# Raw weights of the second down block of a pair in four plain tiles of 128x512 instead of two tiles of 128x1024

## The chip, the cores and the metric

The kernel runs on one core of a Trainium2 chip. The metric is device time in microseconds (us), the median of several runs; lower is better. The engines are TensorE (PE in the profile, its weight loads PEld), VectorE (DVE), ScalarE (ACT), GpSimd (POOL) and SyncE (SP), which here only issues DMAs.

## The reference

Two transformer layers on 512 tokens of width 1024, in fp32. Each layer has a mixing part (layer 0: chunked spatial gating; layer 1: attention with forgetting over 12 heads; both beside an attention over 256 memory rows), and then a feed-forward part with 2816 hidden columns, which is what matters here:

```
f = rmsnorm(h, ln_ffn_pre[layer])
f = (silu(f @ w_ffn_gate[layer]) * (f @ w_ffn_up[layer])) @ w_ffn_down[layer]
h = h + rmsnorm(f, ln_ffn_post[layer])
```

## The kernel before

Every fp32 matrix product is made of three matmuls. An operand is split into a high part (`whi`, a cast to fp32r by ScalarE) and a low part (`wlo`, the difference, by VectorE); `mm3` (L191 to L193) adds high x high, high x low and low x high in PSUM. The splits of L239 are the largest groups of ScalarE and VectorE.

The 22 hidden blocks of 128 columns of a layer are worked off as two in front and then five groups of four (`groups`). In a group, blocks go in pairs. A pair is a gate block and an up block, each of the class `Seven`: a 2x2 block product made of seven half-size products instead of eight, with sums of weights (L1040, L1042, L1044, L1045, on VectorE) before the products. A `Seven` loads its raw weights at L144 into two tiles of 128x1024 with the tag `raw`. Its products run in the order 1, 7, 6, 2, 5, 4, 3; product 1 goes to the PSUM tile `a`, product 7 to the tile `e` (tag `tr`, two banks), others to `x`, and ScalarE copies partial results from PSUM to PSUM at L1055. The ends of a gate block are sums on VectorE (L1083, L1084), a product with the row scale (L1171) and a Silu on ScalarE (L1172).

When the two pairs of a group are done, in the first four groups of a layer, `down_sevens` multiplies their 512 hidden columns with the down weights, again as products of seven: a `DownSeven` `a` for the first pair and a `DownSeven` `b` for the second. Results gather in the eight accumulators `ys` (plain tiles `y` of 128x512): by an addition on VectorE (`final`, L1265), or by a copy on ScalarE (`put`, L1260) and an accumulating DMA from GpSimd's queue (L1262, `y<-yo`). Sums of partial results between PSUM banks are copied by ScalarE (L1286). There are eight such stages in all, four in each layer. In the fifth group of a layer the down weights go through the ordinary tail, which is not part of the change.

The pools that matter:
- `raw`: four tiles of 128x1024 fp32, used in turn by every `Seven` (two each) and every `DownSeven` (two each);
- `y` (function `plain`): twelve tiles of 128x512 fp32. Eight are the accumulators; the other four hold nothing in the groups of layer 1 and, in layer 0, the raw memory rows `mem` for layer 1, which are loaded at L345 and read by ScalarE and VectorE (L243, L244) in the last group;
- the weight parts: eight tiles each of high and low parts, from which TensorE reads.

A `DownSeven` reads its raw weights for the sums L1235, L1237, L1239 and L1240 on VectorE, and cuts seven weight tiles into parts from them and the sums, each just ahead of its product. So a raw tile comes free when the last part is cut from it, in the middle of the stage. Both its loads stand in SyncE's queue, in which a load whose tile is not free holds up the loads behind it.

A planner orders the instructions of each engine at build time, by the order in which they are written and by costs that it assumes, with the waits on tiles and data; at run time each engine works its list off in order. The program text is thus a list of priorities, not the order of issue.

Of the kernel before, what the change touches and what calls it, by code (L numbers as in the profile page):

```python
# [7 lines left out]
F32 = mybir.dt.float32  # L8
# [7 lines left out]
P = 128  # L16
# [24 lines left out]
def hybrid(ctx: ExitStack, tc: tile.TileContext, i: dict, out: bass.AP):  # L41
    nc = tc.nc
# [4 lines left out]
    wp = ctx.enter_context(tc.tile_pool(name="weights", bufs=4))  # L47
# [5 lines left out]
    last_load, last_exp, last_parts = [None], [None], [None, None]  # L53

    def name(s):
        n_of[s] = n_of.get(s, 0) + 1
        return f"{s}_{n_of[s]}"
# [4 lines left out]
    def plain(s, shape=(P, T), dt=F32):  # L62
        return yp.tile(list(shape), dt, tag="y", name=name(s))

    def prob(s, shape=(P, T)):
        return tp.tile(list(shape), F32, tag="p", name=name(s), bufs=6)

    def temp(s, shape=(P, T), tag="t", bufs=4, dt=F32):
        return tp.tile(list(shape), dt, tag=tag, name=name(s), bufs=bufs)
# [4 lines left out]
    def ps(tag, shape=(P, T), s="ps"):  # L74
        return pp.tile(list(shape), F32, tag=tag, name=name(s), bufs=2 if tag == "tr" else 3)
# [1074 lines left out]
    def feed_forward(layer, phase, xp, meanwhile=None):  # L1150
# [43 lines left out]
        class Inner:  # L1194

            def __init__(self, k, aside):
                self.k, self.aside, self.u = k, aside, {}
# [22 lines left out]

        class DownSeven:

            def __init__(self, pair):
                self.x = pair.x
                raws = []
                for dh in range(2):
                    raw = wp.tile([P, 1024], F32, tag="raw", name=name("raw"), bufs=4)
                    last_load[0] = nc.sync.dma_start(
                        raw.rearrange("p (m c) -> p m c", m=4),
                        i["w_down"][layer, 4 * dh : 4 * dh + 4, :, pair.k : pair.k + 2, :].rearrange("m p k c -> p m (k c)"))  # L1230
                    raws.append(raw.rearrange("p (m k c) -> p m k c", m=4, k=2))
                a11, a12, a21, a22 = (r[:, :, x, :] for r in raws for x in range(2))
                self.w = {4: a22}
                s3 = temp("s3").rearrange("p (m c) -> p m c", m=4)
                V.tensor_sub(s3, a11, a21)  # L1235
                self.w[1] = self.parts(a11)
                V.tensor_add(a21, a21, a22)  # L1237
                self.w[2] = self.parts(a12)
                V.tensor_sub(a11, a11, a21)  # L1239
                V.tensor_add(a12, a11, a12)  # L1240
                self.w.update({3: a12, 5: a21, 6: a11, 7: s3})
# [14 lines left out]
        def down_sevens(pairs):  # L1256

            def put(x, *where):
                some = prob("yo")
                A.copy(some, x)  # L1260
                for tb, dh in where:
                    G.dma_start(ys[tb][dh], some, accum_op=ALU.add)  # L1262

            def final(x, tb, dh):
                V.tensor_add(ys[tb][dh], x, ys[tb][dh])  # L1265

            a, b = DownSeven(pairs[0]), None
            chain = [ps("lg", s="yc") for _ in range(2)]
            a.product(chain, 1, True, False)
            lows = [ps("mm", s="yl") for _ in range(2)]  # L1270
            a.product(lows, 2, True, False)
            shared = [ps(t, s="ys") for t in ("tr", "tr")]
            a.product(shared, 7, True, False)
            ups = [ps(t, s="yu") for t in ("mm", "lg")]
            a.product(ups, 3, True, False)
            b = DownSeven(pairs[1])
            b.product(chain, 1, False, True)
            for x in range(2):
                put(chain[x], (x, 0))
            b.product(shared, 7, False, True)  # L1280
            for x in range(2):
                put(shared[x], (x, 1), (x + 2, 1))
            for u in (a, b):
                u.product(chain, 6, False, u is b)
            for x in range(2):
                A.copy(shared[x], chain[x])  # L1286
            b.product(ups, 3, False, True)
            for x in range(2):
                final(ups[x], x + 2, 0)
            a.product(chain, 5, False, False)  # L1290
            a.product(shared, 4, False, False)
            b.product(lows, 2, False, True)
            for x in range(2):
                final(lows[x], x, 0)
            b.product(chain, 5, False, True)
            for x in range(2):
                put(chain[x], (x + 2, 0), (x + 2, 1))
            b.product(shared, 4, False, True)
            for x in range(2):
                final(shared[x], x, 1)  # L1300
# [11 lines left out]
        a, close = boundary(phase, G_MIX_POST + layer, G_FFN_PRE + layer, nnorm, rb, first, evac_first, scaled)  # L1312
# [12 lines left out]
        for gi, (k0, k1) in enumerate(groups):  # L1325
            fs, pairs = [], []
            for m in range(k0, k1, 2):
                if meanwhile and m == k1 - 2 and gi == len(groups) - 1:
                    next(meanwhile)
                if gi < len(groups) - 1:  # L1330
                    pairs.append(Inner(m, m < k1 - 2))
                else:
                    fs += [(act("fhi"), act("flo")) for _ in range(2)]
                Kind = FirstSeven if m == 2 else Seven
                sevens((lambda: Kind(xs, lambda n: i["w_gate"][layer, m + n], gate_rows),
                        lambda: Kind(xs, lambda n: i["w_up"][layer, m + n],
                                     lambda row, src, t: up_rows(row, src, t, fs, pairs and pairs[-1]))), m == 2, m == k0)
            nk = k1 - k0
            if gi == len(groups) - 1:
                if layer:  # L1340
                    with behind([gates[2]]):
                        A.preload_act_table_set("natural_log_exp_and_others")
                if meanwhile:
                    next(meanwhile)

                eps = small("eps")
                V.tensor_mul(eps, nnorm.r4, nnorm.r4)
                V.reciprocal(eps, eps)
                V.tensor_scalar_mul(eps, eps, RMS_EPS)
                return tail_of(fs, lambda kp, dh, aside, k0=k0: down_weights(layer, k0 + 2 * kp, dh, aside), ys, eps,  # L1350
                               layer == 1)
            down_sevens(pairs)
# [300 lines left out]
```

## Time and profile before

| | |
|---|---|
| time, median of 3 runs (lowest to highest) | 1120.58 us (1119.38 to 1121.08) |
| profiled execution | 1125.12 us; span 1123.4 us |
| mean granted TensorE clock | 0.989 |
| busy: TensorE, weight loads, VectorE, ScalarE, GpSimd | 1091.1, 995.8, 956.2, 760.7, 107.7 us |
| loads of down weights | 44 of 512 KB, 4.3 us from issue to landing (median) |
| accumulating DMAs y<-yo | 80 of 256 KB, 8.1 us (median) |
| loads of gate weights by a Seven or ahead | 44 of 512 KB, 4.0 us (median) |

A line of the groups or of the timeline names the source line, the engine, the operation, the tiles written and read (out<-in), the shapes and the count; in brackets, or behind the second bar, stands the idle time of the engine just before it and what ended that. A busy TensorE in the profile is not TensorE at its peak, since matmul ends are modelled. The windows give busy time by engine in the order TensorE, weight loads, VectorE, ScalarE, GpSimd, and then the granted clock, the DMA engines' busy share and GB/s.

### The profile page before, as it was taken

How to read it: one execution, taken by the hardware profiler on the slowest of the kernel's cores; microseconds unless marked ns; L12 is line 12 of the kernel's file. 1: busy time of each engine (PE TensorE's matmuls, PEld its weight loads, DVE VectorE, ACT ScalarE, POOL GpSimd, SP SyncE). 2: the span in 40 equal slices, each digit the busy share in tenths (PEclk: the TensorE clock that was granted, in tenths of full speed). 3: DMA queues.
4: the chain of work that ended last, by engine and by line, in shares of the span. 5: the costliest groups of instructions: out<-in, count | busy, mean ns of one | idle time of the engine just before them, and what ended most of it. 6: DMA issues, size and time to landing. Idle time of an engine off the chain costs nothing.

```text
span 1123.4 us, 19912 instructions
## 1 busy us (share of the span) xinstructions
PE 1091.1 (97%) x7267; PEld 995.8 (89%) x7267; DVE 956.2 (85%) x1906; ACT 760.7 (68%) x1588; POOL 107.7 (10%) x136
## 2 busy tenths in 40 slices
PE   9999999999999999899999999999999999999898
PEld 7998889998989899898988998889988989889896
DVE  7879769998989889896868889779998989979876
ACT  6776578666657657577646888788666657657464
POOL 0000000002030202101000000010012030202100
PEclk9999999999999999999999999999999999989999
DMA  7521331338475655755222555331238485644732
GB/s 264 152 85 57 113 113 39 114 93 208 131 174 163 142 141 130 171 167 155 76 76 76 153 138 139 100 113 39 94 77 211 127 182 157 150 132 120 181 95 76
DMA packets 77850, 143.85 MB, mean 128 GB/s; under 512 B 6772, under 2 KB 41608, under 8 KB 77752
## 3 DMA queue, kind: packets, MB, share of 16 engines
q1 hardware_dynamic: 63032, 116.57, 33.6%
q0 software_dynamic: 14016, 25.70, 13.3%
q8 instruction: 57, 0.93, 0.4%
q10 hardware_dynamic: 704, 0.32, 0.1%
q14 instruction: 41, 0.34, 0.1%
HBM read 105.23 MB, written 2.10 MB: 96 GB/s over the span
## 4 chain that ended last, share of the span: by engine, by line
PE 60%; DVE 18%; DMA 13%; issue 4%; ACT 4%; POOL 1%; DVEq 0%; SPq 0%; ACTq 0%
DVE wlo L239 6%; DMA raw<-in_w_gate 5%; PE y L191 4%; PE y L192 4%; PE y L193 4%; DMA y<-yo 4%; PE ps L191 4%; PE ps L193 4%; PE ps L192 4%; DMA raw<-in_w_down 3%; PE a L191 3%; PE a L193 2%; PE a L192 2%; PE v L191 2%; PE v L193 2%
## 5 line engine op out<-in xcount | busy, mean ns | idle before, releaser
L239 ACT CAST whi<-raw 128x512 fp32r<-128x512 f32 x492 | 293.1, 619 | 149.9 <-PE x L192 28.5
L239 DVE TENSOR_TENSOR wlo<-raw,whi 128x512 fp32r<-128x512 f32 x492 | 326.4, 684 | 30.9 <-ACT whi L239 29.3
L191 PE MATMUL a<-xshi,whi 128*128 128x256 f32 x320 | 90.8, 284 | 1.1 <-ACT e L1055 1.1
L191 PE MATMUL x<-xshi,whi 128*128 128x256 f32 x320 | 91.6, 286 | 0.3 <-ACT x L1055 0.3
L193 PE MATMUL x<-xshi,wlo 128*128 128x256 f32 x320 | 90.9, 284 | 0.0
L192 PE MATMUL x<-xslo,whi 128*128 128x256 f32 x320 | 90.9, 284 | 0.0
L193 PE MATMUL a<-xshi,wlo 128*128 128x256 f32 x320 | 90.0, 281 | 0.0
L192 PE MATMUL a<-xslo,whi 128*128 128x256 f32 x320 | 90.0, 281 | 0.0
L1262 POOL DMA_DIRECT2D y<-yo x80 | 69.6, 1263 | 210.9 <-ACT yo L1260 182.8
L191 PE MATMUL ps<-xshi,whi 128*128 128x256 f32 (+1 forms) x224 | 68.4, 305 | 0.0
L192 PE MATMUL ps<-xslo,whi 128*128 128x256 f32 (+1 forms) x224 | 66.6, 298 | 0.0
L193 PE MATMUL ps<-xshi,wlo 128*128 128x256 f32 (+1 forms) x224 | 66.3, 298 | 0.0
L191 PEld LDWEIGHTS a<-xshi,whi 128*128 128x128 f32 x320 | 60.6, 189 | 2.6 <-ACT e L1055 2.2
L191 PEld LDWEIGHTS x<-xshi,whi 128*128 128x128 f32 x320 | 61.8, 193 | 1.0 <-ACT x L1055 0.9
L192 PEld LDWEIGHTS x<-xslo,whi 128*128 128x128 f32 x320 | 61.5, 192 | 0.0
L193 PEld LDWEIGHTS x<-xshi,wlo 128*128 128x128 f32 x320 | 61.4, 192 | 0.0
L192 PEld LDWEIGHTS a<-xslo,whi 128*128 128x128 f32 x320 | 60.5, 189 | 0.4
L193 PEld LDWEIGHTS a<-xshi,wlo 128*128 128x128 f32 x320 | 60.4, 189 | 0.0
L1040 DVE TENSOR_TENSOR s<-raw,raw 128x512 f32<-128x512 f32 x40 | 27.5, 688 | 36.4 <-DMA raw<-in_w_gate 32.4
L191 PE MATMUL e<-t3hi,whi 128*128 128x256 f32 x160 | 46.0, 287 | 12.5 <-ACT whi L239 6.7
L191 PE MATMUL a<-d2hi,whi 128*128 128x256 f32 x160 | 48.2, 302 | 9.1 <-ACT x L1055 9.1
L239 ACT CAST whi<-s 128x512 fp32r<-128x512 f32 x56 | 34.8, 621 | 31.1 <-DVE s L1040 16.2
(359 smaller groups left out, 3598.4 us busy)
## 6 DMA issues: line engine op xcount, KB each, us to landing
raw<-in_w_gate SPq DMA_DIRECT2D x44, 512.0 KB, 4.0
raw<-in_w_up SPq DMA_DIRECT2D x44, 512.0 KB, 4.6
raw<-in_w_down SPq DMA_DIRECT2D x44, 512.0 KB, 4.3
y<-yo POOLq DMA_DIRECT2D x80, 256.0 KB, 8.1
raw<-in_w_out SPq DMA_DIRECT2D x16, 512.0 KB, 4.0
flo<-s POOLq DMA_DIRECT2D x16, 256.0 KB, 3.4
raw<-in_w_b_q SPq DMA_DIRECT2D x8, 512.0 KB, 4.8
raw<-in_w_a_v SPq DMA_DIRECT2D x6, 512.0 KB, 8.2
```

The lines of the kernel that those rows point to most:

```text
L191: PE.matmul(o, w[0], x[0], start=start, stop=False, skip_group_check=more)
L192: PE.matmul(o, w[0], x[1], start=False, stop=False, skip_group_check=more)
L193: return PE.matmul(o, w[1], x[0], start=False, stop=stop, skip_group_check=more)
L239: last_parts[:] = A.copy(hi, src), (eng or V).tensor_sub(lo, src, hi)
L1040: V.tensor_add(self.s3, a11, a21)
L1262: G.dma_start(ys[tb][dh], some, accum_op=ALU.add)
```

## The change

`DownSeven` takes a second argument. The first block of a stage loads as before: two loads of 512 KB into two `raw` tiles, in rows of 1 KB, with the two weight blocks of the pair interleaved. The second block takes four tiles `wd` from the pool `y` instead, one for each quarter of the weights (a11, a12, a21, a22), and fills them by four loads of 256 KB in rows of 512 bytes. All sums, splits and products stay, on tiles that are contiguous instead of strided.

```diff
         class DownSeven:
 
-            def __init__(self, pair):
+            def __init__(self, pair, spare):
                 self.x = pair.x
-                raws = []
-                for dh in range(2):
-                    raw = wp.tile([P, 1024], F32, tag="raw", name=name("raw"), bufs=4)
-                    last_load[0] = nc.sync.dma_start(
-                        raw.rearrange("p (m c) -> p m c", m=4),
-                        i["w_down"][layer, 4 * dh : 4 * dh + 4, :, pair.k : pair.k + 2, :].rearrange("m p k c -> p m (k c)"))
-                    raws.append(raw.rearrange("p (m k c) -> p m k c", m=4, k=2))
-                a11, a12, a21, a22 = (r[:, :, x, :] for r in raws for x in range(2))
+                if spare:
+                    a11, a12, a21, a22 = (plain("wd").rearrange("p (m c) -> p m c", m=4) for _ in range(4))
+                    for n, a in enumerate((a11, a12, a21, a22)):
+                        last_load[0] = nc.sync.dma_start(
+                            a, i["w_down"][layer, 4 * (n // 2) : 4 * (n // 2) + 4, :, pair.k + n % 2, :].rearrange("m p c -> p m c"))
+                else:
+                    raws = []
+                    for dh in range(2):
+                        ...
+                    a11, a12, a21, a22 = (r[:, :, x, :] for r in raws for x in range(2))
...
-            a, b = DownSeven(pairs[0]), None
+            a, b = DownSeven(pairs[0], False), None
...
-            b = DownSeven(pairs[1])
+            b = DownSeven(pairs[1], True)
```

More of the change, by code (lines that the diff above doesn't have):

```diff
@@ L1221, in feed_forward @@
         class DownSeven:
-            def __init__(self, pair):
+            def __init__(self, pair, spare):
                 self.x = pair.x
-                raws = []
-                for dh in range(2):
-                    raw = wp.tile([P, 1024], F32, tag="raw", name=name("raw"), bufs=4)
-                    last_load[0] = nc.sync.dma_start(
-                        raw.rearrange("p (m c) -> p m c", m=4),
-                        i["w_down"][layer, 4 * dh : 4 * dh + 4, :, pair.k : pair.k + 2, :].rearrange("m p k c -> p m (k c)"))
-                    raws.append(raw.rearrange("p (m k c) -> p m k c", m=4, k=2))
-                a11, a12, a21, a22 = (r[:, :, x, :] for r in raws for x in range(2))
+                if spare:
[6 more added lines that the diff above has]
+                    for dh in range(2):
+                        raw = wp.tile([P, 1024], F32, tag="raw", name=name("raw"), bufs=4)
+                        last_load[0] = nc.sync.dma_start(
+                            raw.rearrange("p (m c) -> p m c", m=4),
+                            i["w_down"][layer, 4 * dh : 4 * dh + 4, :, pair.k : pair.k + 2, :].rearrange("m p k c -> p m (k c)"))
+                        raws.append(raw.rearrange("p (m k c) -> p m k c", m=4, k=2))
+                    a11, a12, a21, a22 = (r[:, :, x, :] for r in raws for x in range(2))
                 self.w = {4: a22}
```

## The prediction

> **What bounds the kernel now.** I read the page first: its span and its chain of work that ended last, by engine.
>
> ```profile
> span 1123.4 us, 19912 instructions
> ...
> PE 60%; DVE 18%; DMA 13%; issue 4%; ACT 4%; POOL 1%; DVEq 0%; SPq 0%; ACTq 0%
> ```
>
> TensorE sets the time, but 18% of the chain is VectorE and 13% is DMA, which can only be places where TensorE stood still. So next: what TensorE waited for (columns: total us, times, longest).
>
> ```profile
> PE a L191 <- ACT x L1055: 9.1, 4, 3.0
> PE e L191 <- ACT whi L239: 6.7, 3, 2.6
> PE e L191 <- DVE y L1265: 5.8, 5, 2.0
> PE ys L192 <- DVE wlo L239: 1.9, 2, 1.5
> ```
>
> Tile e belongs to the second product of a gate block. Its eight waits (6.7 + 5.8 = 12.5 us) are one for each of the eight stages of down blocks, right behind them: the first gate block of the next group. The four waits of tile a (9.1 us) come later in that group. Behind VectorE's part stands a load:
>
> ```profile
> DVE s L1040 <- DMA raw<-in_w_gate: 32.4, 15, 3.9
> ```
>
> The timelines of VectorE and of TensorE (start, length, in brackets the idle time before) behind the first stage, and behind the seventh, shows how one becomes the other.
>
> ```profile
> 262.10 0.69 DVE L1040 TENSOR_TENSOR s<-raw,raw 128x512 f32<-128x512 f32 x1 [3.26 <-DMA raw<-in_w_gate]
> ...
> 266.92 1.28 DVE L1265 TENSOR_TENSOR y<-ys,y 128x512 f32<-128x512 f32 x2
> ...
> 990.59 0.69 DVE L1040 TENSOR_TENSOR s<-raw,raw 128x512 f32<-128x512 f32 x1 [3.32 <-DMA raw<-in_w_gate]
> ```
>
> ```profile
> 267.75 0.36 PE L191 MATMUL e<-t3hi,whi 128*128 128x256 f32 x1 [2.02 <-ACT whi L239]
> ...
> 996.54 0.58 PE L191 MATMUL a<-d2hi,whi 128*128 128x256 f32 x1 [2.69 <-ACT x L1055]
> ```
>
> VectorE runs in order. At 262.10 it had stood 3.26 us at the first sum of the next gate block; the additions of L1265, which free the PSUM bank that e needs, and the parts of e's weights stood behind that, and TensorE lost 2.02 us. At 990.59 the same happens to the second gate block of a group: the sums that end the first gate block (L1084) and the Silu on ScalarE come late, and ScalarE's copy of a (L1055) stands behind that Silu: 2.69 us of TensorE. Now the DMA queue of SyncE, where the load was late:
>
> ```profile
> 228.57 9.89 SPq L1228 DMA_DIRECT2D raw<-in_w_down  x3
> 253.59 1.51 SPq L144 DMA_DIRECT2D raw<-in_w_gate  x2
> ...
> 963.71 2.18 SPq L144 DMA_DIRECT2D raw<-in_w_gate  x2
> ...
> 979.29 4.13 SPq L144 DMA_DIRECT2D raw<-in_w_gate  x2
> ```
>
> Four tiles called raw go round in pairs. The last down load leaves at 238.5; the gate load has to wait for the first pair's down tiles and leaves at 253.59. By then the accumulating DMAs to y fill the engines (the second window below: DMA share, the column before the last, 1.01), and it lands only at 262.
>
> ```profile
> 238.50:242.50 4.00, 4.00 (x36) 4.00 (x35) 4.00 (x8) 1.50 (x5) 0.00 (x0) 1.00 0.90 265
> 253.00:262.20 9.20, 9.20 (x41) 7.40 (x40) 5.59 (x10) 5.44 (x11) 4.32 (x5) 1.00 1.01 236
> ```
>
> **The change part by part.**
>
> *The pair of raw tiles that the second down block gives up.* The next gate block now takes the two tiles that the second down block took: free from about 238, since that block's own loads left then (228.57 + 9.89). The gate load goes some 15 us earlier, ahead of the accumulating DMAs, and by the two down loads of 238.5, which kept the engines for 0.90 x 4.0 = 3.6 us, it lands near 243 instead of 262. Its wait at L1040 goes. Late next is the bank of e: VectorE must have done L1265. Two stages show it with hardly a load in the way:
>
> ```profile
> 456.42 0.35 PE L191 MATMUL e<-t3hi,whi 128*128 128x256 f32 x1 [0.30 <-DVE y L1265]
> ...
> 1048.02 0.35 PE L191 MATMUL e<-t3hi,whi 128*128 128x256 f32 x1 [0.55 <-DVE y L1265]
> ```
>
> I take their mean, 0.42, for all eight: 3.4 us stay of 12.5, a gain of 9.1 (bounds: 8 x 0.30 left, 10.1; 8 x 0.55 left, 8.1).
>
> *The clock behind the waits.* Windows right behind five waits, granted clock in the third column from the end:
>
> ```profile
> 268.60:272.05 3.45, 3.45 (x19) 3.45 (x19) 3.45 (x7) 1.93 (x4) 0.86 (x1) 0.52 1.12 203
> 394.80:398.30 3.50, 3.50 (x20) 3.50 (x19) 3.50 (x7) 0.90 (x3) 0.40 (x1) 0.53 1.09 228
> 920.50:924.10 3.60, 3.60 (x20) 3.60 (x19) 3.60 (x7) 0.99 (x2) 1.33 (x2) 0.53 1.10 167
> 997.00:1002.60 5.60, 5.60 (x28) 5.60 (x28) 3.98 (x7) 2.33 (x6) 0.00 (x0) 0.50 0.15 60
> 1063.80:1067.40 3.60, 3.60 (x20) 3.60 (x19) 3.53 (x6) 1.36 (x5) 0.00 (x0) 0.53 0.09 35
> ```
>
> The first three follow waits for e: 3.45 x 0.48 + 3.50 x 0.47 + 3.60 x 0.47 = 5.0 us lost, which go with the waits (bounds 0 and 5.0). The last two follow waits of tile a: 5.60 x 0.50 + 3.60 x 0.47 = 4.5 us. [...]
>
> *The second gate block of a group* (four waits of a, 9.1 us, and 4.5 us of clock: 13.6). Its loads wait for the first gate block's tiles, as before (979.29 and 4.13 us on), and the accumulating DMAs still run. Two things pull: the wait that now exists in four stages shrinks, because VectorE no longer stands at the first gate load before it; but it shows where the first gate block is early, and the change makes that so in all eight. Bounds: all 13.6 gained, or the same price, 13.6 / 4 = 3.4, in all eight, 13.6 lost. I take the middle, 0, since the seventh stage (first gate load at 963.71, 15 us before the second's at 979.29; 3.32 us of wait for the second) speaks for the loss and VectorE's shorter backlog for the gain.
>
> *The second block's own loads.* Four of 256 KB into tiles y, waiting for no raw tile: right behind the eight accumulators' own allocation, and then each time the block before has used its tiles up, most of the 62 us from one stage to the next ahead of use. In the first stage of a layer VectorE no longer waits for them and TensorE's wait at ys (1.9 us) may shrink: 1.0 taken, bounds 0 and 1.9.
>
> *What it adds.* Two more issues on SyncE per stage, at a third of a microsecond (tile mem between 100 and 600; min, median and max ns):
>
> ```profile
> L243 ACT ACTIVATE mparts<-mem,gains x8: 493/494/510, 482.0 to 485.1; 128x256 fp32r<-128x256 f32 x8
> ...
> L345 SPq DMA_DIRECT2D mem<-in_mem x4: 327/328/328, 195.4 to 198.9; - x4
> ```
>
> 2 x 0.33 = 0.7 us, covered by a queue that waits 15 us between 238.5 and 253.59. If the cover went, the loads behind are 0.7 us later, 5.6 us at most in all. Packets halve to 512 bytes.
>
> ```profile
> q1 hardware_dynamic: 63032, 116.57, 33.6%
> ```
>
> Of the row of SyncE's queue (packets, MB, share of 16 engines): a 1 KB packet of a down load took 3.6 x 16 / 1024 = 56 ns, the mean packet (1.85 KB) 0.336 x 1123.4 x 16 / 63032 = 96 ns, so about 7 ns plus 48 per KB, an estimate: 31 ns for 512 bytes, 4.0 us per block for 3.6, covered by the same lead: 0; if all the time were per packet, 3.6 us more a block, still under that lead. [...] VectorE's operations keep their count and 128x512 shape: 0. In the first layer those four tiles held mem from 195 to 485. Mem now loads when the fourth stage ends, by 456, some 26 us before its use: 0, and if that cover failed, one load's landing, about 4 us.
>
> *VectorE's room.* Eight windows from stage to stage (busy TensorE, loads, VectorE, ScalarE, GpSimd): the fullest and the sum.
>
> ```profile
> 919.60:982.00 62.40, 60.94 (x420) 57.06 (x421) 59.44 (x106) 42.34 (x83) 11.72 (x14) 0.97 0.66 157
> ...
> sum 504.40, PE 485.29 PEld 451.02 DVE 461.86 ACT 328.43 POOL 80.92; mean PE 60.66 PEld 56.38 DVE 57.73 ACT 41.05 POOL 10.12
> ```
>
> The fullest leaves 2.96 us, the mean 63.05 - 57.73 = 5.3. A gain of 15.1 / 8 = 1.9 fits. I charge 1.0 in all for VectorE's tighter order.
>
> **Sum.** 9.1 + 5.0 + 0 + 1.0 - 1.0 = 14.1 us. The profiled execution took 1125.12 (1.7 around its span), 4.5 above the median 1120.58; the gain is taken off the median: 1106.5.
>
> **The rivals.**
> - *The wait only moves.* The second gate block stalls in all eight stages at the mean price: 8 x 3.4 + 3.4 left = 30.6, for 12.5 + 5.0 + 13.6 + 1.0 = 32.1 now. Time 1119. For it: the seventh stage as it is. Against: without the wait at the first gate load the first gate block's tiles come free earlier, and the second's load with them.
> - *Slower, by the same place.* If each of the eight costs what 996.54 cost (2.69 + 2.8 of clock = 5.5), it is 44 + 3.4 = 47.4: 15 us slower, 1136. It decides from (32.1 - 3.4) / 8 = 3.6 us a stage. Against: only one of four costs that much now.
> - *Everything goes.* The second gate block's wait too: 9.1 + 5.0 + 1.9 + 13.6 = 29.6, 1091. Against: 3.7 us a stage is more than the fullest window has.
> - *The change doesn't do what it says*: the four tiles are not empty, mem keeps them in the first layer, and the first layer gains nothing: half the gain, 7 us, 1113.5.
>
> **Chances.** Forecast (8 to 20 us faster, 1100.5 to 1112.5) 0.52; everything 0.14; half the gain or a small one 0.09; the wait moves 0.13, of which 0.09 within 0.2% (2.2 us, about what this kernel's runs can tell apart) and 0.03 above it; slower 0.12. Faster 0.78, same 0.09, slower 0.13. The range leaves out the slower case above 1121 (0.13) and the far end of the best below 1095 (0.05); the likeliest case alone is 1100 to 1113.
>
> **What would show it.** Right: the first gate load of a group leaves near the last load of the first down block, not 15 us behind it; no wait of 3 us at L1040 behind a down stage; waits for e near 0.4; clock 1.0 behind them. Wrong: waits of tile a at L1055 in more than four stages, or L1040 waiting for the second gate load near 3 us; then the loads that wait for the first gate block's tiles, not the down tiles, set the stage. Also wrong: a wait for the tiles wd.

## The result and the profile after

The changed kernel takes 1103.72 us (median of 4 runs, 1101.56 to 1106.95); the kernel before, in the same rounds, 1119.98 (4 runs, 1116.04 to 1121.08). The ratio is 0.986, interval 0.983 to 0.990: 16.3 us or 1.5% faster. The profiled execution after is the fastest of its runs (1101.56, span 1099.8), that of before (1125.12) lies 5.1 above its median; so the two traces differ by 23.6 us where the medians differ by 16.3.

The chain of the kernel after by engine, from its page, and what TensorE waited for (total us, times, longest):

```profile
PE 75%; DVE 9%; DMA 7%; issue 4%; ACT 3%; POOL 1%; SPq 0%; DVEq 0%; ACTq 0%; POOLq 0%
```

```profile
PE a L191 <- ACT x L1055: 9.8, 6, 2.1
PE a L191 <- ACT e L1055: 2.5, 4, 1.0
```

VectorE's share of the chain has halved from 18%, DMA's nearly from 13%. The waits of tile e (12.5 us, eight of them) and of ys (1.9 us) are gone from the list. The waits of tile a behind ScalarE's copy of x are still there: 9.1 us in four before, 9.8 us in six now, none as long as the longest before (3.0). SyncE's queue shows why the waits of e are gone, in the stretch in which before's gate load left at 253.59:

```profile
221.47 5.62 SPq L1234 DMA_DIRECT2D raw<-in_w_down  x2
235.62 0.94 SPq L144 DMA_DIRECT2D raw<-in_w_gate  x2
251.27 0.33 SPq L144 DMA_DIRECT2D raw<-in_w_up  x1
251.83 0.98 SPq L1228 DMA_DIRECT2D wd<-in_w_down  x2
254.24 0.34 SPq L144 DMA_DIRECT2D raw<-in_w_up  x1
254.84 3.29 SPq L1228 DMA_DIRECT2D wd<-in_w_down  x2
266.35 1.41 SPq L144 DMA_DIRECT2D raw<-in_w_gate  x2
```

The first gate load leaves at 235.62, 18 us earlier than before. Now the up load waits for the first pair's down tiles. The four loads of wd, for the stage after this one, stand between and behind its two halves, each as soon as the tile's last part is cut, and leave beside the accumulating DMAs (DMA share 1.09 between 253 and 266 us). VectorE's waits for DMAs:

```profile
DVE s L1040 <- DMA raw<-in_w_gate: 14.6, 8, 2.8
...
DVE y L1271 <- DMA y<-yo: 6.1, 5, 1.5
```

14.6 us for gate loads instead of 32.4. New are 6.1 us at L1271 (L1265 before), where an addition to y must wait for an accumulation to the same y; before, two such waits came to 0.8. They differ from execution to execution: the next profiled one of the same kernel, in the first experiment, has 2.7 us in two.

What is left of the old pattern is best seen behind the third stage of layer 1, in the timelines of VectorE, ScalarE and TensorE (start, length; in brackets the idle time before):

```profile
971.75 0.69 DVE L1040 TENSOR_TENSOR s<-raw,raw 128x512 f32<-128x512 f32 x1 [2.43 <-DMA raw<-in_w_gate]
...
974.16 0.42 DVE L1084 TENSOR_TENSOR s<-a,s 128x256 f32<-128x256 f32 x1
...
975.43 0.69 DVE L1171 TENSOR_TENSOR s<-s,rbc 128x512 f32<-128x512 f32 x1
976.03 0.69 DVE L1171 TENSOR_TENSOR s<-x,rbc 128x512 f32<-128x512 f32 x1
```

```profile
976.15 1.23 ACT L1172 ACTIVATE s<-s 128x512 f32<-128x512 f32 x2 [2.50 <-DVE s L1171]
977.28 0.36 ACT L1055 COPY x<-a 128x256 f32<-128x256 f32 x1
```

```profile
977.70 0.39 PE L191 MATMUL a<-d2hi,whi 128*128 128x256 f32 x1 [1.78 <-ACT x L1055]
```

VectorE stands 2.43 us at the first sum of the *second* gate block, whose matmuls start only at 986.45, some 15 us later. The sums that end the first one stand behind it, then its two products with the row scale (L1171), which the two Silus (L1172) wait for, then, in ScalarE's order, a copy that TensorE needs at once.

### The profile page after: what moved, and what is told of

It reads as the page before. It is cut to its first block, busy times and chain, and to the rows that moved or that the text cites. A ratio compares the mean times of both kernels' runs of the same rounds, so it can differ in the third digit from the quotient of the medians.

```text
span 1099.8 us, 19894 instructions
## 1 busy us (share of the span) xinstructions
PE 1080.4 (98%) x7266; PEld 986.5 (90%) x7267; DVE 955.7 (87%) x1906; ACT 760.6 (69%) x1588; POOL 107.7 (10%) x136
## 4 chain that ended last, share of the span: by engine, by line
PE 75%; DVE 9%; DMA 7%; issue 4%; ACT 3%; POOL 1%; SPq 0%; DVEq 0%; ACTq 0%; POOLq 0%
PE y L191 5%; PE y L192 5%; PE y L193 5%; PE ps L191 4%; DMA y<-yo 4%; PE ps L193 4%; PE ps L192 4%; PE a L191 4%; PE a L192 3%; PE a L193 3%; DVE wlo L239 3%; DMA raw<-in_w_gate 3%; PE x L191 2%; PE x L192 2%; PE x L193 2%
## 5 line engine op out<-in xcount | busy, mean ns | idle before, releaser
L239 ACT CAST whi<-raw 128x512 fp32r<-128x512 f32 x444 | 266.2, 619 | 131.3 <-PE x L192 26.2
L239 DVE TENSOR_TENSOR wlo<-raw,whi 128x512 fp32r<-128x512 f32 x444 | 296.4, 686 | 27.2 <-ACT whi L239 25.6
L191 PE MATMUL y<-whi,mixedhi 128*128 128x512 f32 x128 | 51.3, 401 | 0.0
L192 PE MATMUL y<-wlo,mixedhi 128*128 128x512 f32 x128 | 50.6, 395 | 0.0
L193 PE MATMUL y<-whi,mixedlo 128*128 128x512 f32 x128 | 50.3, 393 | 0.0
## 6 DMA issues: line engine op xcount, KB each, us to landing
wd<-in_w_down SPq DMA_DIRECT2D x32, 256.0 KB, 10.8
```

The costliest lines, as they stand in the source:

```text
L191: PE.matmul(o, w[0], x[0], start=start, stop=False, skip_group_check=more)
L192: PE.matmul(o, w[0], x[1], start=False, stop=False, skip_group_check=more)
L193: return PE.matmul(o, w[1], x[0], start=False, stop=stop, skip_group_check=more)
L239: last_parts[:] = A.copy(hi, src), (eng or V).tensor_sub(lo, src, hi)
```

## The experiments

Theory 1: the gain is the pair of raw tiles, which the next gate block finds free. Theory 2: it is the second block's own weights, early and contiguous. Theory A for what is left: VectorE's order, which puts a sum with a late load ahead of urgent work. Ratios are to the kernel before.

**The change again** (ratio 0.985, 0.982 to 0.987; 1103.66 us).

> The changed kernel once more, beside the others on one chip. Both theories: 1103.7 us, some 16 us under the kernel before (ratio 0.986).

As expected; it is the yardstick for the three that shared its chip.

**Two raw tiles still taken.** A tiny load into each, and a tiny copy out of each at parts 3 and 4:

```diff
+                    for dh in range(2):
+                        raw = wp.tile([P, 1024], F32, tag="raw", name=name("raw"), bufs=4)
+                        nc.sync.dma_start(raw[:, :8], i["w_down"][layer, 4 * dh, :, pair.k, :8])
+                        self.held.append(raw)
...
+                if self.held and n in (3, 4):
+                    A.copy(small("held", 8), self.held[n - 3][:, :8])
```

> The changed kernel, but the second down block still takes two raw tiles (filled by loads of a few bytes) and lets go of them where it did before, so the next gate load waits again; its weights lie in the four plain tiles as in the change. Theory 1 (the gain is the pair of raw tiles that the next gate block finds free): the gain goes, 1116 to 1120 us, with first gate loads again some 15 us behind the last down load and waits of tile e near 12 us in all. Theory 2 (the gain is the second block's own early weights, contiguous and without a wait for raw tiles): 1103 to 1106 us, waits of e near 0.

1104.64 us, 0.985 (0.982 to 0.988). By the text that is theory 2, but the edit failed to do what it says. SyncE's queue:

```profile
235.39 0.94 SPq L1229 DMA_DIRECT2D raw<-in_w_down  x2
237.64 0.80 SPq L144 DMA_DIRECT2D raw<-in_w_gate  x2
```

The gate load leaves 2 us behind the tiny loads: the copies hung on nothing but them, so the planner put them early (the first two run at 237.43) and the tiles came free. Nothing follows for either theory. (It does show that the tiny loads and copies cost nothing that can be seen: 1104.64 against 1103.66.)

**Held until the parts are cut.** The same, but the part writes into the held tile, so the tile can't come free before it:

```diff
-                    A.copy(small("held", 8), self.held[n - 3][:, :8])
+                    A.copy(self.held[n - 3][:, :8], w[0][:, :8].bitcast(F32))
```

> The changed kernel, but the second down block again holds two raw tiles, now until its parts 3 and 4 are cut (a few elements of the part are copied into the raw tile, so it can't come free earlier, as the first attempt did); its weights lie in the plain tiles as in the change. Theory 1 (the freed raw pair is the gain): first gate loads about 15 us behind the last down load again, waits of tile e back near 12 us, 1116 to 1121 us. Theory 2 (the second block's own early weights are the gain): 1103 to 1106 us, waits of e near 0.

1131.9 us, 1.009 (1.006 to 1.011): slower than before the change, and outside the ranges of both theories. SyncE's queue and TensorE's waits:

```profile
235.11 0.94 SPq L1229 DMA_DIRECT2D raw<-in_w_down  x2
250.75 1.01 SPq L144 DMA_DIRECT2D raw<-in_w_gate  x2
253.29 4.00 SPq L144 DMA_DIRECT2D raw<-in_w_up  x2
257.34 6.90 SPq L1233 DMA_DIRECT2D wd<-in_w_down  x4
```

```profile
PE a L191 <- ACT x L1055: 23.4, 11, 4.5
PE e L191 <- DVE y L1278: 10.2, 6, 3.1
```

With the tiles held the gate load leaves at 250.75 again, the waits of e are back at 10.2 us, and those of a have more than doubled. All weights of the second block lie in the plain tiles as in the change, and the gain is gone, so theory 2 does not carry it. But that it is 10 us *worse* than before was not expected, and so the run has a cost of its own; the next one asks why.

**Held, and the wd loads ahead of the stage.** With the two tiles held, the wd loads go behind the first block's loads in SyncE's queue (the edit is that of the next experiment).

> The fifth experiment (two raw tiles still held until parts 3 and 4 are cut) with the loads of wd behind the first block's own loads in SyncE's queue. Theory (the fifth ran 10 us slower than the kernel before because the wd loads stood among the gate and up loads of the next group, in the stretch of the accumulating DMAs): the excess goes, 1117 to 1123 us, as before the change. Rival (the held tiles or the small copies cost by themselves): 1128 us and above.

1116.44 us, 0.997 (0.995 to 0.999). TensorE's waits:

```profile
PE a L191 <- ACT x L1055: 15.2, 6, 3.4
PE e L191 <- DVE y L1280: 5.2, 3, 2.0
```

The excess is gone, and a little more. So the wd loads cost some 13 us (the ratios differ by 0.012; the two ran on different chips) where they stand among gate and up loads that are already late, and the held tiles and copies are not the source of that excess. Whether the wd loads cost by their place in SyncE's queue or by their share of the DMA engines is not separated.

This run is also the clean test of theory 1. The next experiment has the same order of loads and no tiles held, and takes 1099.34 us (ratio 0.980): holding the pair costs some 17 us by the medians, the whole gain of the change, and brings waits of e back. With the pair still held, the plain, contiguous tiles gain some 4 us over the kernel before (1116.44 against 1120.44). So freeing the pair is the gain, and theory 2 has a small share of it at most.

**The wd loads out of the crowded stretch**, in the changed kernel:

```diff
-                        last_load[0] = nc.sync.dma_start(
-                            a, ...)
+                    with behind([last_load[0]]):
+                        for n, a in enumerate((a11, a12, a21, a22)):
+                            last = nc.sync.dma_start(a, ...)
+                    last_load[0] = last
```

> The changed kernel, with the four loads of wd put behind the first block's own loads in SyncE's queue, so they leave in the quiet stretch ahead of the stage and no longer in the crowded one behind the stage before. Theory 1: the freed raw pair does it all, so the time stays, 1102 to 1105 us, or gains up to 3 us where the second gate load finds an emptier queue. Theory 2 (the second block's early weights matter): VectorE waits for them again at its first sum, 2 to 3 us slower than the changed kernel, 1106 to 1107 us.

1099.34 us (1097.41 to 1101.56), 0.980 (0.978 to 0.983): 4.3 us under the changed kernel by medians, though the two intervals touch. VectorE's waits and TensorE's:

```profile
DVE s L1040 <- DMA raw<-in_w_gate: 17.4, 8, 3.5
DVE y L1273 <- DMA y<-yo: 1.6, 1, 1.6
```

```profile
PE a L191 <- ACT x L1055: 10.1, 6, 2.4
PE a L191 <- ACT e L1055: 1.0, 1, 1.0
```

It gains somewhat more than the 3 us that theory 1 allowed, and not by the way that it said: the wait for the gate load is no shorter (17.4, against 14.6 and 16.4 in the two profiled executions of the changed kernel). The wait for accumulations is shorter, but by how much is unsure (1.6, against 6.1 in one and 2.7 in the other). TensorE's waits of a come to 11.1 us, against 13.5 in the execution of the changed kernel on the same chip, and the spans of these two differ by the same 2.4 us (1098.7 and 1101.1). Where the rest of the 4.3 us comes from, if it is more than noise, stays open. Where the early lead of a stage is given up, nothing is lost: VectorE does not wait for wd.

**The sums of the second gate block behind the end of the first**, on VectorE:

```diff
-                with behind(ended if opens else ()):
+                with behind(ended if opens else ends[-2:-1] if second and u is not None and make is pair[0] else ()):
                     u.sums()
...
                 u.end()
+                ends.append(ended[0])
```

(`second` is true for the second pair of a group that stands behind a stage of down blocks.)

> The changed kernel, with the sums of the second gate block of a group ordered on VectorE behind the end of the first gate block (its product with the row scale), so that a late load no longer holds up that end. Theory A (the 9.8 us of waits of tile a are VectorE standing in order at L1040 for the second gate load): waits of a fall under 3 us and the time to 1094 to 1098 us. Rival B (the second gate block needs its weights by then, so the wait moves to its own first parts, or VectorE has no room to do the sums later): 1102 to 1107 us, with waits of about the same sum in other places.

1089.33 us (1087.85 to 1090.85), 0.971 (0.968 to 0.974): 14.3 us under the changed kernel, more than the 9.8 us of waits and 1.6 us of clock that it was to save, and below the range of theory A. In TensorE's waits the whole row of a behind x is gone, with nothing in its place:

```profile
PE a L191 <- ACT e L1055: 2.1, 5, 0.5
```

No load got faster; only the order changed, so theory A holds. The saving fits the two executions that shared a chip: TensorE's waits of a fall from 13.5 us (11.1 behind x, 2.4 behind e) to 2.1, and the mean granted clock of the runs rises from 0.996 to 1.000 (medians), some 4 us of 1103 by an estimate.

**The same order in the kernel before.**

> The kernel before, with only the order on VectorE of the fourth experiment: the sums of the second gate block behind the end of the first. Theory (two separate waits, one for each gate block of a group): the waits of tile a (9.1 us and 4.5 us of clock) go, those of e (12.5 and 5.0) stay, 1106 to 1111 us. Rival (one wait, which shows now at one block, now at the other): the waits of e grow by what a loses, 1116 to 1121 us.

1109.9 us, 0.990 (0.987 to 0.992).

```profile
PE e L191 <- ACT whi L239: 7.4, 3, 2.9
PE e L191 <- DVE y L1266: 6.2, 5, 2.1
PE ys L192 <- DVE wlo L239: 2.0, 2, 1.6
```

The waits of a are gone, those of e stay (13.6 us against 12.5). So there were two waits, one for each gate block of a group; the change took away the one, the order takes away the other.

**Without the accumulating DMAs.** The changed kernel, 80 DMAs of 256 KB less, and the results that they add missing from the output:

```diff
-                for tb, dh in where:
-                    G.dma_start(ys[tb][dh], some, accum_op=ALU.add)
```

> The changed kernel without its 80 accumulating DMAs: the partial results that they add to y are left out of the output. Theory C (the second gate load lands late because the accumulating DMAs crowd the engines): its time from issue to landing falls from 7 to under 4 us, VectorE's waits at L1040 and L1271 go, 1090 to 1094 us. Rival (it is late because its tiles come free late): the waits of tile a stay near 10 us, 1100 to 1104 us.

1084.23 us, 0.967 (0.965 to 0.970).

```profile
DVE s L1040 <- DMA raw<-in_w_gate: 0.9, 2, 0.7
```

Faster than either theory had it. 14.6 us at L1040 fall to 0.9, and the waits of a are gone from TensorE's list. The second gate load of a group leaves about as long after the first as before (29.2 to 29.5 us here, 29.2 to 30.7 in the changed kernel; its second half up to 1.6 us earlier), so the rival falls. What changes is the landing: of the gate loads whose landing the traces show, the slowest takes 4.1 us here and 7.7 in the changed kernel (medians 3.9 and 4.1). Theory C holds: most of the lateness is crowding. How much of the 19 us comes from the earlier landing, and how much from VectorE's waits at L1271 that go as well, is not separated.

**The two edits that gained, together.**

> The third and the fourth experiment together. If the late loads of wd gain by sparing the stretch of the accumulating DMAs (VectorE's waits at L1271), that gain is separate from the order of the sums: 1085 to 1088 us. If it came from the second gate load landing earlier, nothing is left of it here: 1088 to 1091 us.

1085.5 us (1084.74 to 1086.35), 0.968 (0.966 to 0.971): the best version, 36.2 us under the kernel before (1121.74 in the same rounds) and 1.3 us from the kernel that leaves the accumulation out. It lies in the range for two separate gains, and VectorE's waits for accumulations (4.9 us with the order of the sums alone) are gone; but the step from that experiment, 0.971 to 0.968 on another chip, is within the intervals.

```profile
PE 95%; DVE 2%; ACT 2%; DMA 0%; issue 0%; SPq 0%; DVEq 0%; ACTq 0%
```

```profile
262.00:322.00 60.00, 60.00 (x428) 56.28 (x427) 59.58 (x107) 43.07 (x84) 11.23 (x14) 1.00 0.67 163
322.00:382.00 60.00, 60.00 (x428) 56.31 (x427) 58.78 (x105) 41.52 (x81) 11.21 (x13) 1.00 0.67 160
382.00:442.00 60.00, 60.00 (x429) 56.28 (x428) 57.00 (x102) 42.03 (x82) 10.72 (x13) 1.00 0.71 178
```

DMA has left the chain. In 60 us windows of the groups TensorE is busy throughout, at the full clock; VectorE follows at 57.0 to 59.6 and is the next fullest, so it would probably be the next to bind.

**Layer 1 alone** (`b = DownSeven(pairs[1], layer == 1)`).

> The change in layer 1 alone; layer 0 as before, so mem stays in its four tiles from 195 us on. If each stage gains by itself and mem's later load costs nothing: half of the 16 us, or by the idle times of TensorE some 9 us in layer 1 and 7 in layer 0, so 1110 to 1113 us. If mem's move costs, or the gain hangs on layer 0: outside that, below 1108 or above 1116 us.

1110.57 us, 0.991 (0.989 to 0.994), 9.9 of the 16 us by medians. The waits of e are left in layer 0 alone (three, 3.9 us, in the timeline of TensorE). So the gain goes by layers, with the larger part in layer 1; the 6.4 us of layer 0 are a difference and not a run, but they leave no room for a large cost of mem's move. Mem now loads from 430.8 and is read from 471.6 in the changed kernel.

## Why the prediction was right

Forecast 1106.5 us, measured 1103.72, from a gain of 14.1 against 16.3. The first step, that the pair of raw tiles goes to the next gate block, is shown by the queue (235.62 instead of 253.59; 15 us ahead were forecast, 18 were measured) and by the held tiles, which undo the gain (1116.44 against 1099.34 with the same order of loads). By terms, in the two profiled executions:

- Waits of e: forecast 12.5 to 3.4, measured 0. The residue taken from 456.42 and 1048.02 was too large: TensorE does not wait for e in any stage. Why those two stages had a residue before is not shown. In its place stand a few waits of a behind the copy of e (2.5 us for 1.1).
- Clock behind the waits of e: 5.0 forecast, and all of it came, since there are no such waits: the clock is 1.00 in the 3.5 us from the first matmul of e on, behind each of the eight stages. But the length of a wait does not decide whether it costs clock. Before, the longest wait of e (2.58 us, before 857.48) cost none, though 2.02 us before 267.75 did:

```profile
858.40:862.00 3.60, 3.60 (x32) 3.56 (x31) 3.60 (x7) 2.71 (x6) 0.86 (x1) 1.00 1.13 208
```

  Windows of the kernel after, behind a wait of 1.78, one of 1.81 and one of 1.56 us:

```profile
977.70:981.90 4.20, 4.20 (x23) 4.20 (x24) 3.98 (x7) 2.18 (x5) 0.00 (x0) 0.61 0.23 89
399.00:402.50 3.50, 3.50 (x31) 3.50 (x31) 3.28 (x7) 2.56 (x6) 0.00 (x0) 1.00 0.24 96
916.20:919.70 3.50, 3.50 (x30) 3.50 (x31) 3.46 (x7) 2.67 (x6) 0.00 (x0) 1.00 0.49 152
```

  The first lost 0.39 x 4.2 = 1.6 us, the others nothing, and neither did the three other waits of a behind x, the longest of all (2.07 us) among them: 1.00 in the 3.5 us behind each. What decides whether a wait costs clock, no run here shows.
- The second gate block: forecast unchanged at 13.6, measured 9.8 + 1.6 = 11.4. The two pulls named were both real: six stages stall now, not four, and each for less. That is one of the signs that the prediction itself had named for being wrong (waits of a in more than four stages), and the longest wait at L1040 (2.8 us) is near the other; the 0 was the middle between two pulls of up to 13.6 us each, so its nearness to 2.2 is in part luck. The rival in which it stalls in all eight at the old price had the right place and the wrong price (1.9 us a stage with its clock, not 3.4).
- The wait at ys: 1.0 of 1.9 forecast, 1.9 came.
- What it adds: taken as covered. VectorE does not wait for wd, so the cover held, with 10.8 us from issue to landing (median) and most of a stage in hand. Yet the loads have a cost by where they stand: some 13 us where the pair is held, and perhaps 4.3 us in the changed kernel, by the medians of the experiment with the wd loads moved. The charge of 1.0 for VectorE's tighter order is not measured by any run.

Sum by the traces: 12.5 - 1.4 + 5.0 + 2.2 + 1.9 = 20.2 us, of 23.6 between the spans; the forecast had 14.1, and the medians gave 16.3. Of the remaining 3.4 us of the spans, 1.7 lie ahead of everything that the change touches (the first load of wd leaves at 193.71): between 8 and 14 us of the execution before the granted clock was 0.72 (6.00 x 0.28), in that of after 1.00. The other 1.7 are not assigned.

The medians differ by less than the traces because the profiled execution before ran at a low clock: 0.989 in the mean, where 37 later executions of the same kernel had 0.989 to 0.997, with a median of 0.993. By an estimate that is 0.004 x 1123 = 4.5 us, most of the 5.1 by which it lies above its median. By medians, then, again an estimate, TensorE's waits of a, e and ys gave 12.3 us (24.6 to 12.3) where the forecast had 9.1, and the clock some 4 us (0.993 to 0.997) where it had 5.0: together the 16 us measured. The two errors have opposite signs and cancel in part.

Gate loads, which stand in SyncE's queue, landed later beside the accumulating DMAs of GpSimd's: without those DMAs the slowest whose landing the traces show took 4.1 us instead of 7.7, and VectorE's waits for gate loads fell from 14.6 to 0.9 us. The forecast had the share of 1.01 in front of it and used it for the first gate load only, not for where the wd loads would go.

## What to carry to other kernels

When users share a pool of buffers, the one worth adding belongs to whoever waits longest for its turn: taking a user out of the pool frees buffers for the *next* user, and that is where to look for the gain. Ask then where the moved loads go: a load that is free to leave at once may leave in a stretch that is already full, as wd did here (DMA share 1.01 between 253 and 262.2 us before the change, 1.09 between 253 and 266 with it). And VectorE worked off its list in order, so that an early sum with a late load held up more than a late sum: ordering it behind urgent work gained nearly as much here (14 us) as the buffers did (16 us), with no load faster.

## What the runs showed that was not expected

- The granted clock behind an idle time of TensorE did not go by the length of that time: 0.61 over 4.2 us behind 1.78 us, and 0.52 over 3.45 us behind 2.02 before the change, but 1.00 behind 2.07, and behind 2.58 before the change.
- The same 1 MB of wd loads a stage, moved by about half of the 60 us from stage to stage, cost some 13 us in all among loads that are late already (ratio 1.009 against 0.997), and perhaps 4 us among loads that are mostly in time (1103.66 against 1099.34, intervals that touch).
